# The head's modulation in columns: weights stationary, one column of c moving

## The chip, the cores and the metric

The kernel runs on one core of one Trainium2 chip. The metric is the device time of one execution in microseconds (us). A core has five engines that run their own queues in order and wait for each other by semaphores: PE (TensorE, the matrix engine; PEld is its loading of weights), DVE (VectorE), ACT (ScalarE), POOL (GpSimd) and SP (SyncE, which here issues nearly all DMA transfers).

## The reference

Two transformer blocks follow each other on 256 tokens of 1024 columns, all in f32. The part that the change touches is the start of the first block: a modulation vector computed from `c`, and the first gated feed-forward layer.

```python
c_act = jax.nn.silu(c)                                                       # (1, 1024)
mod = (einsum('bd,dn->bn', c_act, w_ada[l]) + b_ada[l]).reshape(b, 3, 3, 1024)
h = rms_norm(x, norm_w[l, 0]) * (1 + mod[:, 0, 1]) + mod[:, 0, 0]            # modulate
x = x + 0.5 * mod[:, 0, 2] * swiglu(h, ffn_w13[l, 0], ffn_w2[l, 0])
# swiglu: g, u = split(h @ w13); (silu(g) * u) @ w2, with 2816 columns of g and of u
```

A mixer with attention and convolution, a second feed-forward layer and the second block follow; `p_2` is an input of the second block, which the kernel transposes early.

## The kernel before

Everything is kept transposed: columns of the model on the 128 partitions, the 256 tokens along the free axis. A product of two f32 matrices is made of three fast products (`mm3`, lines 154 to 156): both operands are split into a rounded part `hi` (ACT, a cast) and the rest `lo` (DVE, a subtraction), by `hilo` (L178, L179) or `split` (L143, L144). In the tables below `gu` is the bank in which g and u of the first feed-forward layer are summed, `acc` that of its second product.

**The head.** `x` comes in, is transposed raw (`xt_ps<-ident,x_nat`) and, once its row norm is known, normed (`xn`). The modulation vector has 9216 columns, of which the first layer needs shift (0 to 1023) and scale (1024 to 2047) at once. They are computed in four blocks of 512 columns: `ada_start(0)` and `ada_start(8)` are shift and scale of the model's first 512 columns, `ada_start(4)` and `ada_start(12)` of the last 512 (the number is the column in units of 128). I call them blocks 0, 8, 4 and 12. Of a block, the 1024 rows of `w_ada` lie as 128 partitions x 8 terms, two tiles `ada` of four terms (1 MB each). Before, terms 0, 1, 4 and 5 are multiplied by their value of c and added up by DVE (`ada_acc`, L216 and L218); terms 2, 3, 6 and 7 go to PE with c as the stationary operand, broadcast over 128 columns, and 512 columns of weights moving (L221); one more product with a matrix of ones adds `ada_acc` over the partitions (L223). The result stands 128 times in a bank `ada_ps`; DVE picks its diagonal, 128 columns at a time, by a multiplication with the identity and a sum (L226, four times), and adds the bias (L228), into columns of `modT`. `ada_scale` (L199) turns the scale into `aT`.

**The first strip.** The first layer goes over 11 strips of 256 columns of g and u. The first strip's weights come in two halves of four terms (`strips_half`), and `h_half(i)` makes four terms of the modulated input h: nu (L592, ACT: `xn` times `aT` plus `modT`), hh and hl (its two parts), and the casts of the half strip between. `gemm_half(i)` multiplies: per term 2 output groups x 2 (g, u) x 3 products. So the strip is 8 terms x 12 = 96 products of 256 columns, and then the second strip's 96 follow (`i = 1` in `swiglu`), then the first down strip.

**What sets the order.** The code is written in the order below; a scheduler in the framework then orders each engine's instructions by its own estimate of when their inputs are there, unless `issue_after` ties one behind another. On the chip each engine goes through its queue strictly in that order. SP's queue issues the transfers in order too; seven tiles `ada` can be held, so the eighth waits for the first. `then` is a list of small jobs, one behind each strip: `vector_columns` loads nine small vectors (`rowB`) and transposes them, `transpose_p` transposes `p_2`.

```python
    ada_start(0, (0, 1, 4, 5))
    ada_start(8, (0, 1, 4, 5))
    strips_half(0)
    h_half(0)
    ada_start(4, (0, 1, 4, 5))
    ada_start(12, (0, 1, 4, 5))
    gemm_half(0)
    strips_half(4)
    h_half(4)
    gemm_half(4)
```

Of the kernel before, what the change touches and what calls it, by code (L numbers as in the profile page):

```python
# [8 lines left out]
F32 = mybir.dt.float32  # L9
# [4 lines left out]
ALU = mybir.AluOpType  # L14
# [4 lines left out]
P = 128  # L19
T = 256  # L20
D = 1024
KD = D // P
# [39 lines left out]
def tile_two_blocks(ctx: ExitStack, tc: tile.TileContext, t: dict, out: bass.AP):  # L62
    nc = tc.nc
    vec, act, pe, sync, pool = nc.vector, nc.scalar, nc.tensor, nc.sync, nc.gpsimd
# [12 lines left out]
    def bankB(name):  # L77
        return psB.tile([P, 512], F32, tag="ps", name=name)
# [21 lines left out]
    start = tc.tile_pool(name="start", bufs=1)  # L100
    start_ctx, start = start, start.__enter__()
# [7 lines left out]
    ident = const.tile([P, P], F32, name="ident")  # L109
# [5 lines left out]
    ones = {}  # L115
# [49 lines left out]
    def gemm_many(jobs, x, kc, ks=None):  # L165

        for k in ks or range(kc):
            for i, (ps, w, c0) in enumerate(jobs):
                mm3(ps, w[0][:, k, c0:c0 + P], w[1][:, k, c0:c0 + P], x[0][:, k, :], x[1][:, k, :],
                    k == 0 and i % 2 == 0, k == kc - 1)  # L170
# [6 lines left out]
    def hilo(src, hi, lo):  # L177
        act.copy(hi, src)  # L178
        vec.tensor_tensor(out=lo, in0=src, in1=hi.bitcast(F32), op=ALU.subtract)  # L179

    def tr(dst, src, n=P):
        pe.transpose(out=dst, in_=src, identity=ident[:n, :n])
# [5 lines left out]
    c_act = const.tile([P, 8], F32, name="c_act")  # L188
    tab(c_act, c_raw, AF.Silu)
    modT = const.tile([P, 72], F32, name="modT")  # L190
    aT = const.tile([P, 24], F32, name="aT")
    gT = const.tile([P, 24], F32, name="gT")
    colA = const.tile([P, 96], F32, name="colA")
    xT = res.tile([P, KD, T], F32, name="xT")
    w_ada = t["w_ada"][0].rearrange("(p k) n -> p k n", k=8)
# [3 lines left out]
        vec.scalar_tensor_tensor(out=aT[:, s * 8 + ci:s * 8 + ci + n], in0=modT[:, s * 24 + 8 + ci:s * 24 + 8 + ci + n],  # L199
                                 scalar=1.0, in1=colA[:, 72 + s * 8 + ci:72 + s * 8 + ci + n], op0=ALU.add, op1=ALU.mult)  # L200

    def ada_start(ci, mine):

        parts = []
        for k0 in (0, 4):
            w = start.tile([P, 2048], F32, tag="ada", name="ada", bufs=7)
            wv = w.rearrange("p (k n) -> p k n", k=4)
            sync.dma_start(out=wv, in_=w_ada[:, k0:k0 + 4, ci * P:ci * P + 512])
            parts += [wv[:, k, :] for k in range(4)]
        acc = start.tile([P, 512], F32, tag="ada_acc", name="ada_acc", bufs=2)  # L210
        b = bankB("ada_ps")
        begun = False
        for k in range(8):
            if k in mine:
                if k == mine[0]:
                    vec.tensor_scalar_mul(acc, parts[k], c_act[:, k:k + 1])  # L216
                else:
                    vec.scalar_tensor_tensor(out=acc, in0=parts[k], scalar=c_act[:, k:k + 1], in1=acc,  # L218
                                             op0=ALU.mult, op1=ALU.add)
            else:  # L220
                pe.matmul(b, lhsT=c_act[:, k:k + 1].to_broadcast([P, P]), rhs=parts[k], start=not begun, stop=False)  # L221
                begun = True
        pe.matmul(b, lhsT=ones[1], rhs=acc, start=False, stop=True)  # L223
        for i in range(4):
            junk = start.tile([P, P], F32, tag="junk", name="junk", bufs=2)
            vec.tensor_tensor_reduce(out=junk, in0=b[:, i * P:(i + 1) * P], in1=ident, scale=1.0, scalar=0.0,  # L226
                                     op0=ALU.mult, op1=ALU.add, accum_out=modT[:, ci + i:ci + i + 1])
        vec.tensor_tensor(out=modT[:, ci:ci + 4], in0=modT[:, ci:ci + 4], in1=colA[:, ci:ci + 4], op=ALU.add)  # L228


    colB = const.tile([P, 64], F32, name="colB")
# [2 lines left out]
    def vector_columns():  # L234
        rowB = tmp.tile([P, P], F32, tag="nu", name="rowB")
        vec.memset(rowB[32:64, :], 1.0)
        at = 0
        for name, v in (("mix", t["norm_mix_g_2"][0]), ("mlp", t["norm_mlp_g_2"][0]), ("ple", t["norm_ple_g_2"][0]),
                        ("bg", t["b_gate_2"][0]), ("qa", t["q_a_norm"][0]), ("kva", t["kv_a_norm"][0]),
                        ("cw", t["conv_w"][0].rearrange("j c -> (j c)"))):  # L240
            n = v.shape[0] // P
            sync.dma_start(out=rowB[at:at + n], in_=v.rearrange("(r c) -> r c", c=P))
            col_at[name] = at
            at += n
        for name, a in (("mq", t["q_norm_nope"]), ("mk", t["k_norm_nope"])):
            sync.dma_start(out=rowB[at:at + 1, 0:64], in_=a)
            col_at[name] = at
            at += 1
        b = bankB("col_ps2")
        tr(b[:, 0:at], rowB[0:at, :], at)  # L250
        vec.tensor_copy(colB[:, 0:at], b[:, 0:at])
# [74 lines left out]
    def drain(g):  # L326
        for _ in g:
            pass
# [43 lines left out]
    def h_tiles():  # L372
        return (res.tile([P, KD, T], F32R, tag="hh", name="hh"), res.tile([P, KD, T], F32R, tag="hl", name="hl"))
# [150 lines left out]
    def transpose_p():  # L524
        pnat = tmp.tile([P, 2, 256], F32, tag="pnat", name="pnat", bufs=1)
        sync.dma_start(out=pnat, in_=t["p_2"][0][0].rearrange("(k p) n -> p k n", p=P))
        b = bankB("pT")
        for c in range(2):
            for tk in range(2):
                tr(b[:, c * T + tk * P:c * T + (tk + 1) * P], pnat[:, tk, c * P:(c + 1) * P])  # L530
        hilo(b, flat(pH), flat(pL))
# [16 lines left out]
    for tk in range(2):  # L548
        junk = start.tile([P, D], F32, tag="xn", name="junk", bufs=2)
# [18 lines left out]
    b = bankB("col_ps")  # L568
# [4 lines left out]
    h = h_tiles()  # L573

    h = h_tiles()
    rope_steps = rope_table()
# [5 lines left out]
    first = [bankB("gu") for _ in range(2)]  # L582
# [12 lines left out]
                for z in range(2):  # L595
                    hilo(part(raw[z], k, 2), part(hi[z], k, 2), part(lo[z], k, 2))

    def gemm_half(i):
        gemm_many([(b[:, z * T:(z + 1) * T], (whole(hi[z]), whole(lo[z])), j * P) for j, b in enumerate(first)
                   for z in range(2)], h, KD, range(i, i + 4))  # L600

    ada_start(0, (0, 1, 4, 5))
    ada_start(8, (0, 1, 4, 5))
    strips_half(0)
    h_half(0)
    ada_start(4, (0, 1, 4, 5))
    ada_start(12, (0, 1, 4, 5))
    gemm_half(0)
    strips_half(4)
    h_half(4)  # L610
    gemm_half(4)
    start_ctx.__exit__(None, None, None)
    swiglu(h, t["ffn_w13"][0][0], t["ffn_w2"][0][0], gt(0), ada_rest(ada_plan[:8], (0, 0, 1, 1, 1, 1, 1, 1, 1, 1)),
           then=(lambda: None, vector_columns, transpose_p, lambda: next(rope_steps), lambda: None,
                 lambda: drain(rope_steps)), first=first, at=(16, 16))
    mid = ada_rest(ada_plan[8:12], (1,), halves=False)


# [331 lines left out]
    h = modulated(nw(2), sh(2))  # L950
# [310 lines left out]
    h, make_rb = gained("mlp")  # L1261
# [20 lines left out]
    with tc.tile_pool(name="px3", bufs=1) as px:  # L1282
# [5 lines left out]
        h, _ = gained("ple", sums=False)  # L1288
        w = t["w_ple_gate_2"][0]
# [17 lines left out]
        for c in range(2):  # L1307
            for tk in range(2):
                junk = px.tile([P, 512], F32, tag="junk", name="junk", bufs=2)
# [49 lines left out]
        for s in range(2):  # L1359
            b = bankB("pg")  # L1360
# [9 lines left out]
        for part, (c0, n) in enumerate(((0, 512), (512, T), (768, T))):  # L1370
            b = bankB("pg")
# [83 lines left out]
```

## Time and profile before

| | |
|---|---|
| median of 3 runs | 1011.21 us |
| lowest, highest | 1010.92, 3466.13 us |
| the profiled execution's time | 1011.66 us |
| its span, first to last instruction | 1009.9 us |
| PE busy | 983.6 us, 97% of the span |
| weight loads busy | 948.8 us, 94% |
| DVE busy | 745.8 us, 74% |
| ACT busy | 557.9 us, 55% |
| mean granted clock of PE | 0.994 of full |

The profile comes from one execution. Times of instructions are counted from the start of its span; what the device time has beyond the span, 1.76 us, lies around it. A timeline row has the start in us, the duration (of the whole group, where several instructions are merged), the engine, the line, the operation with output and inputs, how many, and in brackets how long the engine had been idle before and what ended that. A duration of PE runs from a product's start to its modelled end, so products overlap, and the distance between starts tells what one costs in a stream.

### The profile page before, as it was taken

How to read it: one execution, taken by the hardware profiler on the slowest of the kernel's cores; microseconds unless marked ns; L12 is line 12 of the kernel's file. 1: busy time of each engine (PE TensorE's matmuls, PEld its weight loads, DVE VectorE, ACT ScalarE, POOL GpSimd, SP SyncE). 2: the span in 40 equal slices, each digit the busy share in tenths (PEclk: the TensorE clock that was granted, in tenths of full speed). 3: DMA queues.
4: the chain of work that ended last, by engine and by line, in shares of the span. 5: the costliest groups of instructions: out<-in, count | busy, mean ns of one | idle time of the engine just before them, and what ended most of it. 6: DMA issues, size and time to landing. Idle time of an engine off the chain costs nothing.

```text
span 1009.9 us, 20118 instructions
## 1 busy us (share of the span) xinstructions
PE 983.6 (97%) x8244; PEld 948.8 (94%) x8244; DVE 745.8 (74%) x1430; ACT 557.9 (55%) x1032; POOL 30.2 (3%) x42
## 2 busy tenths in 40 slices
PE   6999999999999998999999999999999999999996
PEld 3799999999988997999999999999999999999996
DVE  4889999847976999796454679986577885655664
ACT  5654545547765655645444555554566774554555
POOL 0000000010000001000000010001000100000000
PEclk9999999999999998999999999999999999999999
DMA  9899999726574888996563454535545896565411
GB/s 343 283 373 355 332 313 316 267 88 188 169 229 127 258 306 266 321 345 201 177 206 128 126 161 129 173 126 159 161 124 170 264 309 194 192 190 195 160 63 42
DMA packets 159330, 215.28 MB, mean 213 GB/s; under 512 B 6350, under 2 KB 125925, under 8 KB 159110
## 3 DMA queue, kind: packets, MB, share of 16 engines
q1 hardware_dynamic: 157442, 212.58, 63.8%
q10 hardware_dynamic: 1796, 1.42, 0.4%
q8 instruction: 64, 1.05, 0.4%
q14 instruction: 28, 0.23, 0.1%
HBM read 210.51 MB, written 3.47 MB: 212 GB/s over the span
## 4 chain that ended last, share of the span: by engine, by line
PE 79%; DVE 12%; ACT 4%; DMA 3%; issue 2%; SPq 0%; DVEq 0%; ACTq 0%
PE gu L154 8%; PE gu L156 8%; PE gu L155 8%; PE acc L154 7%; PE acc L155 7%; PE acc L156 6%; DVE lo L144 4%; PE u L154 3%; PE u L155 3%; PE u L156 3%; ACT hi L143 2%; DMA ada<-in_w_ada_dram 1%; PE gab L156 1%; DVE ada_acc L274 1%; PE gab L154 1%
## 5 line engine op out<-in xcount | busy, mean ns | idle before, releaser
L144 DVE TENSOR_TENSOR lo<-raw,hi 128x512 fp32r<-128x512 f32 (+2 forms) x454 | 395.2, 900 | 84.1 <-ACT hi L143 83.1
L143 ACT CAST hi<-raw 128x512 fp32r<-128x512 f32 (+2 forms) x454 | 337.0, 786 | 173.4 <-PE acc L155 51.3
L154 PE MATMUL gu<-hh,hi 128*128 128x256 f32 x704 | 198.1, 282 | 3.0 <-ACT hh L385 3.0
L156 PE MATMUL gu<-hh,lo 128*128 128x256 f32 x704 | 195.8, 279 | 0.2 <-DVE lo L144 0.2
L155 PE MATMUL gu<-hl,hi 128*128 128x256 f32 x704 | 195.4, 278 | 0.0
L155 PE MATMUL acc<-ml,hi 128*128 128x256 f32 x608 | 168.0, 277 | 0.4 <-DVE ml L179 0.4
L154 PE MATMUL acc<-mh,hi 128*128 128x256 f32 x608 | 167.9, 278 | 0.3 <-ACT mh L178 0.3
L156 PE MATMUL acc<-mh,lo 128*128 128x256 f32 x608 | 167.8, 277 | 0.0
L154 PEld LDWEIGHTS gu<-hh,hi 128*128 128x128 f32 x704 | 133.5, 190 | 3.6 <-ACT hh L385 3.1
L156 PEld LDWEIGHTS gu<-hh,lo 128*128 128x128 f32 x704 | 133.3, 190 | 0.5 <-DVE lo L144 0.4
L155 PEld LDWEIGHTS gu<-hl,hi 128*128 128x128 f32 x704 | 133.3, 190 | 0.5 <-issue 0.5
L154 PEld LDWEIGHTS acc<-mh,hi 128*128 128x128 f32 x608 | 113.9, 188 | 0.9 <-ACT mh L178 0.7
L155 PEld LDWEIGHTS acc<-ml,hi 128*128 128x128 f32 x608 | 114.0, 188 | 0.8 <-DVE ml L179 0.8
L156 PEld LDWEIGHTS acc<-mh,lo 128*128 128x128 f32 x608 | 114.1, 188 | 0.0
L274 DVE SCALAR_TENSOR_TENSOR ada_acc<-ada,c_act,ada_acc 128x512 f32<-128x512 f32 x98 | 73.4, 749 | 2.1 <-DMA ada<-in_w_ada_dram 0.3
L154 PE MATMUL u<-hh,hi 128*128 128x256 f32 x256 | 71.0, 277 | 0.0
L155 PE MATMUL u<-hl,hi 128*128 128x256 f32 x256 | 70.8, 277 | 0.0
L156 PE MATMUL u<-hh,lo 128*128 128x256 f32 x256 | 70.8, 276 | 0.0
L88 ACT ACTIVATE s<-gu 128x256 f32<-128x256 f32 x44 | 16.6, 379 | 68.3 <-PE gu L156 68.1
L154 PEld LDWEIGHTS u<-hh,hi 128*128 128x128 f32 x256 | 48.1, 188 | 0.0
L155 PEld LDWEIGHTS u<-hl,hi 128*128 128x128 f32 x256 | 48.0, 188 | 0.0
L156 PEld LDWEIGHTS u<-hh,lo 128*128 128x128 f32 x256 | 48.1, 188 | 0.0
(404 smaller groups left out, 2154.0 us busy)
## 6 DMA issues: line engine op xcount, KB each, us to landing
raw<-in_ffn_w_dram SPq DMA_DIRECT2D x64, 1024.0 KB
raw<-in_w_in_dram SPq DMA_DIRECT2D x37, 1024.0 KB
raw<-in_w_ff_dram SPq DMA_DIRECT2D x32, 1024.0 KB
ada<-in_w_ada_dram SPq DMA_DIRECT2D x28, 1024.0 KB
raw<-in_w_out_dram SPq DMA_DIRECT2D x8, 1024.0 KB
ada<-in_w_ada_dram SPq DMA_DIRECT2D x8, 768.0 KB
raw<-in_w_branch_dram SPq DMA_DIRECT2D x8, 512.0 KB
raw<-in_w_out_a_dram SPq DMA_DIRECT2D x4, 1024.0 KB
```

The source lines that it names most:

```text
L88: last_table[0] = act.activation(*args, **kw).ins
L143: act.copy(hi[:, sl], raw[:, sl])
L144: vec.tensor_tensor(out=lo[:, sl], in0=raw[:, sl], in1=hi[:, sl].bitcast(F32), op=ALU.subtract)
L154: pe.matmul(ps, lhsT=wh, rhs=xh, start=start, stop=False, skip_group_check=True)
L155: pe.matmul(ps, lhsT=wh, rhs=xl, start=False, stop=False, skip_group_check=True)
L156: pe.matmul(ps, lhsT=wl, rhs=xh, start=False, stop=stop, skip_group_check=True)
L274: vec.scalar_tensor_tensor(out=acc, in0=wv[:, k, :], scalar=c_act[:, k0 + k:k0 + k + 1], in1=acc, op0=ALU.mult, op1=ALU.add)
```

## The change

`ada_start` now gives the first four terms of a block to DVE and the last four to PE. On PE the weights are the stationary operand, 128 columns at a time, and one column moves: c's value of that term (or a column of ones for `ada_acc`). The result comes as one column per group of 128, four columns of the bank, so the diagonal is no longer read; DVE adds the bias right from the bank. The second tile of block 12 comes in two transfers. The first strip's products are cut 3 + 1 + 4 terms in place of 4 + 4: three terms ahead of blocks 4 and 12, the fourth tied behind block 12's last product. `transpose_p` moves from behind the third strip to behind the second, beside `vector_columns`.

```diff
-    def ada_start(ci, mine):
-
-        parts = []
+    def ada_start(ci, rows=4):
+
+
+        wv = []
         for k0 in (0, 4):
...
+            n = rows if k0 else 4
+            for k in range(0, 4, n):
+                sync.dma_start(out=w[:, k:k + n, :], in_=w_ada[:, k0 + k:k0 + k + n, ci * P:ci * P + 512])
+            wv += [w[:, k, :] for k in range(4)]
         acc = start.tile([P, 512], F32, tag="ada_acc", name="ada_acc", bufs=2)
+        for k in range(4):
+            if k == 0:
+                vec.tensor_scalar_mul(acc, wv[0], c_act[:, 0:1])
+            else:
+                vec.scalar_tensor_tensor(out=acc, in0=wv[k], scalar=c_act[:, k:k + 1], in1=acc, op0=ALU.mult, op1=ALU.add)
         b = bankB("ada_ps")
...
-                pe.matmul(b, lhsT=c_act[:, k:k + 1].to_broadcast([P, P]), rhs=parts[k], start=not begun, stop=False)
-                begun = True
-        pe.matmul(b, lhsT=ones[1], rhs=acc, start=False, stop=True)
-        for i in range(4):
-            junk = start.tile([P, P], F32, tag="junk", name="junk", bufs=2)
-            vec.tensor_tensor_reduce(out=junk, in0=b[:, i * P:(i + 1) * P], in1=ident, scale=1.0, scalar=0.0,
-                                     op0=ALU.mult, op1=ALU.add, accum_out=modT[:, ci + i:ci + i + 1])
-        vec.tensor_tensor(out=modT[:, ci:ci + 4], in0=modT[:, ci:ci + 4], in1=colA[:, ci:ci + 4], op=ALU.add)
+        terms = [(acc, ones[1][:, 0:1])] + [(wv[k], c_act[:, k:k + 1]) for k in range(4, 8)]
+        for n, (w, v) in enumerate(terms):
+            for j in range(4):
+                last = pe.matmul(b[:, j:j + 1], lhsT=w[:, j * P:(j + 1) * P], rhs=v, start=n == j == 0, stop=n == 4,
+                                 skip_group_check=True)
+        vec.tensor_tensor(out=modT[:, ci:ci + 4], in0=b[:, 0:4], in1=colA[:, ci:ci + 4], op=ALU.add)
+        return last.ins
...
-    def gemm_half(i):
+    def gemm_part(i, n):
...
-                   for z in range(2)], h, KD, range(i, i + 4))
-
-    ada_start(0, (0, 1, 4, 5))
-    ada_start(8, (0, 1, 4, 5))
+                   for z in range(2)], h, KD, range(i, i + n))
+
+    ada_start(0)
+    ada_start(8)
     strips_half(0)
     h_half(0)
-    ada_start(4, (0, 1, 4, 5))
-    ada_start(12, (0, 1, 4, 5))
-    gemm_half(0)
+    gemm_part(0, 3)
+    ada_start(4)
+    with tc.issue_after(ada_start(12, rows=2)):
+        gemm_part(3, 1)
     strips_half(4)
     h_half(4)
-    gemm_half(4)
+    gemm_part(4, 4)
...
-           then=(lambda: None, vector_columns, transpose_p, lambda: next(rope_steps), lambda: None,
-                 lambda: drain(rope_steps)), first=first, at=(16, 16))
+           then=(lambda: None, lambda: (vector_columns(), transpose_p()), lambda: None, lambda: next(rope_steps),
+                 lambda: None, lambda: drain(rope_steps)), first=first, at=(16, 16))
```

What the scheduler makes of it on DVE, between the norm of x and the first parts of h, before (block 0's reading of the diagonal, `ISA junk,modT`, and block 8's products; `waits PE_49` is a wait for PE):

```order
L216 TENSOR_SCALAR ada_acc<-ada,c_act 128x512 [waits DMAHW1_49]
L218 SCALAR_TENSOR_TENSOR ada_acc<-ada,c_act,ada_acc 128x512 [waits DVE_49]
L226 ISA junk,modT<-ada_ps,ident 128x128 [waits PE_49]
L226 ISA modT 128x1
...
L228 TENSOR_TENSOR modT<-modT,colA 128x4 [waits DVE_49]
L218 SCALAR_TENSOR_TENSOR ada_acc<-ada,c_act,ada_acc 128x512 [waits DMAHW2_49]
```

and after, from the end of block 0's products to the end of block 12 (L224 is the addition of the bias, L215 and L217 are the products):

```order
L224 TENSOR_TENSOR modT_100<-ada_ps_196,colA_103 128x4 [waits PE_49]
L215 TENSOR_SCALAR ada_acc_222<-ada_218,c_act_98 128x512 [waits DMAHW1_49]
L217 SCALAR_TENSOR_TENSOR ada_acc_222<-ada_218,c_act_98,ada_acc_222 128x512 [waits DVE_49] x3
L224 TENSOR_TENSOR modT_100<-ada_ps_227,colA_103 128x4 [waits PE_49]
L199 SCALAR_TENSOR_TENSOR aT_101<-modT_100,colA_103 128x4 [waits DVE_49]
...
L179 TENSOR_TENSOR hl_178<-nu_272,hh_177 128x256 [waits Activation_49]
L215 TENSOR_SCALAR ada_acc_316<-ada_312,c_act_98 128x512 [waits DMAHW5_49]
L217 SCALAR_TENSOR_TENSOR ada_acc_316<-ada_312,c_act_98,ada_acc_316 128x512 [waits DVE_49] x3
L224 TENSOR_TENSOR modT_100<-ada_ps_321,colA_103 128x4 [waits PE_49]
L215 TENSOR_SCALAR ada_acc_348<-ada_343,c_act_98 128x512 [waits DMAHW7_49]
```

All four products of a block now stand behind the wait for the block before it (two of them did before), and blocks 4 and 12 stand behind the last hl of the first half of h, where before block 4's first product stood among the parts of the strip.

On ACT, behind the two normings of x, before (the casts of the half strip, then nu):

```order
L178 CAST hi<-raw 128x512 [waits DMAHW3_49]
L178 CAST hi<-raw 128x512
L178 CAST hi<-raw 128x512 [waits DMAHW4_49]
L178 CAST hi<-raw 128x512
L592 ACTIVATE nu<-xt_ps,modT,aT 128x256 [waits DVE_49,PE_49]
```

and after (nu is L589 there):

```order
L589 ACTIVATE nu<-xt_ps,modT,aT 128x256 [waits DVE_49,PE_49]
L589 ACTIVATE nu<-xt_ps,modT,aT 128x256
L178 CAST hh<-nu 128x256 [waits Activation_49]
L178 CAST hi<-raw 128x512 [waits DMAHW3_49]
L178 CAST hh<-nu 128x256 [waits Activation_49]
```

The casts have moved from ahead of nu to behind it, and so behind its wait for DVE.

On PE the products of blocks 4 and 12 stood ahead of the first gu products and among them; after, 36 gu products come first, then the two blocks, the second behind the first:

```order
L156 MATMUL gu<-hh,lo 128x256
L222 MATMUL ada_ps<-ones_92,ada_acc 128x1 [waits DVE_49,PE_49]
L222 MATMUL ada_ps<-ones_92,ada_acc 128x1 x3
L222 MATMUL ada_ps<-c_act,ada 128x1 [waits DMAHW6_49]
L222 MATMUL ada_ps<-c_act,ada 128x1 x15
L222 MATMUL ada_ps<-ones_92,ada_acc 128x1 [waits DVE_49,PE_49]
```

A block is 20 products in the program, 4 of `ada_acc` and 16 of the tile.

## Rows read from the trace of the kernel before

**Rows 1.** Windows: busy us by engine, clock, DMA share, GB/s.

```profile
20.00:24.00 4.00, 1.54 (x5) 0.50 (x4) 3.22 (x14) 2.01 (x5) 0.00 (x0) 1.00 1.05 387
...
36.00:40.00 4.00, 4.00 (x38) 4.00 (x37) 3.14 (x15) 1.78 (x6) 0.00 (x0) 1.00 0.60 159
```

**Rows 2.** Timeline of PE: start, us, what; head of the program.

```profile
23.89 1.95 PE L221 MATMUL ada_ps<-ada,c_act 128*128 128x512 f32 x4 [2.46 <-DMA ada<-in_w_ada_dram]
...
31.60 0.68 PE L154 MATMUL gu<-hh,hi 128*128 128x256 f32 x1
...
35.23 0.69 PE L154 MATMUL gu<-hh,hi 128*128 128x256 f32 x1
...
45.40 0.28 PE L156 MATMUL gu<-hh,lo 128*128 128x256 f32 x1
```

**Rows 3.** Timeline of weight loads, same columns.

```profile
11.79 0.19 PEld L221 LDWEIGHTS ada_ps<-ada,c_act 128*128 128x128 f32 x1 [0.43 <-issue]
...
13.54 0.14 PEld L182 LDWEIGHTS xt_ps<-ident,xn 128*128 128x128 f32 x1 [0.26 <-ACT xn L557]
```

**Rows 4.** Source L221: min/median/max ns of one.

```profile
L221 PEld LDWEIGHTS ada_ps<-ada,c_act x32: 185/190/338, 10.0 to 33.9; 128*128 128x128 f32 x32
L221 PE MATMUL ada_ps<-ada,c_act x32: 590/592/1193, 10.0 to 34.3; 128*128 128x512 f32 x32
```

**Rows 5.** Timeline of weight loads, 393 to 396 us.

```profile
394.73 0.52 PEld L909 LDWEIGHTS bias_ps<-hot,wide_tabs 33*128 33x128 f32 x4 [0.33 <-DVE lo L144]
```

**Rows 6.** Source L285: loads of bf16 weights, one column moving.

```profile
L285 PEld LDWEIGHTS <-ada_b x168: 95/96/100, 96.9 to 496.0; 128*128 128x128 bf16 x168
L285 PE MATMUL ada_ps<-one,ada_b x168: 163/163/178, 96.9 to 496.0; 128*128 128x1 bf16 x168
```

**Rows 7.** Timeline of PE, 98 us.

```profile
98.46 0.40 PE L285 MATMUL ada_ps<-one,ada_b 128*128 128x1 bf16 x10
```

**Rows 8.** Source L1187: loads of 64 columns.

```profile
L1187 PEld LDWEIGHTS bob<-pT,vB x64: 132/137/137, 703.2 to 730.9; 128*64 128x64 f32 x64
```

**Rows 9.** Timeline of PE, at 6 us.

```profile
6.01 3.62 PE L182 MATMUL xt_ps<-ident,x_nat 128*128 128x128 f32 x16
```

**Rows 10.** Timeline of PE, from 398 us.

```profile
398.33 1.23 PE L154 MATMUL gu<-hh,hi 128*128 128x256 f32 x4 [2.98 <-ACT hh L385]
...
399.79 0.41 PE L154 MATMUL gu<-hh,hi 128*128 128x256 f32 x1
400.00 0.41 PE L155 MATMUL gu<-hl,hi 128*128 128x256 f32 x1
```

**Rows 11.** Windows around a fall of the clock (columns as in rows 1).

```profile
397.00:398.00 1.00, 0.00 (x0) 0.00 (x0) 0.96 (x3) 0.23 (x1) 0.00 (x0) 0.70 1.11 332
...
404.00:405.00 1.00, 1.00 (x10) 1.00 (x9) 1.00 (x2) 0.21 (x1) 0.00 (x0) 0.88 0.38 82
```

**Rows 12.** Timeline of DVE, head of the program.

```profile
15.35 0.49 DVE L216 TENSOR_SCALAR ada_acc<-ada,c_act 128x512 f32<-128x512 f32 x1 [1.09 <-DMA ada<-in_w_ada_dram]
...
17.18 0.29 DVE L226 CUSTOM_DVE_ANT_0 junk<-ada_ps,ident 128x128 f32<-128x128 f32 x1 [0.56 <-PE ada_ps L223]
...
18.15 0.16 DVE L228 TENSOR_TENSOR modT<-modT,colA 128x4 f32<-128x4 f32 x1
...
27.74 1.53 DVE L218 SCALAR_TENSOR_TENSOR ada_acc<-ada,c_act,ada_acc 128x512 f32<-128x512 f32 x2
29.21 0.49 DVE L216 TENSOR_SCALAR ada_acc<-ada,c_act 128x512 f32<-128x512 f32 x1
29.74 0.75 DVE L218 SCALAR_TENSOR_TENSOR ada_acc<-ada,c_act,ada_acc 128x512 f32<-128x512 f32 x1
```

**Rows 13.** Timeline of ACT, head of the program.

```profile
19.58 1.14 ACT L178 CAST hi<-raw 128x512 fp32r<-128x512 f32 x2 [6.09 <-DMA raw<-in_ffn_w_dram]
...
23.85 1.02 ACT L592 ACTIVATE nu<-xt_ps,modT,aT 128x256 f32<-128x256 f32 x2 [1.63 <-DVE aT L199]
...
25.72 1.02 ACT L592 ACTIVATE nu<-xt_ps,modT,aT 128x256 f32<-128x256 f32 x2 [0.25 <-DVE hl L179]
```

More of the change, by code (lines that the diff above doesn't have):

```diff
@@ L200, in ada_scale @@
                                  scalar=1.0, in1=colA[:, 72 + s * 8 + ci:72 + s * 8 + ci + n], op0=ALU.add, op1=ALU.mult)
-    def ada_start(ci, mine):
-        parts = []
+    def ada_start(ci, rows=4):
+        wv = []
         for k0 in (0, 4):
[L206 to L209, printed above, removed]
-        acc = start.tile([P, 512], F32, tag="ada_acc", name="ada_acc", bufs=2)
-        b = bankB("ada_ps")
[L212 to L220, printed above, removed]
-                pe.matmul(b, lhsT=c_act[:, k:k + 1].to_broadcast([P, P]), rhs=parts[k], start=not begun, stop=False)
-                begun = True
-        pe.matmul(b, lhsT=ones[1], rhs=acc, start=False, stop=True)
-        for i in range(4):
-            junk = start.tile([P, P], F32, tag="junk", name="junk", bufs=2)
-            vec.tensor_tensor_reduce(out=junk, in0=b[:, i * P:(i + 1) * P], in1=ident, scale=1.0, scalar=0.0,
-                                     op0=ALU.mult, op1=ALU.add, accum_out=modT[:, ci + i:ci + i + 1])
-        vec.tensor_tensor(out=modT[:, ci:ci + 4], in0=modT[:, ci:ci + 4], in1=colA[:, ci:ci + 4], op=ALU.add)
@@ new lines, in ada_start @@
+            w = start.tile([P, 2048], F32, tag="ada", name="ada", bufs=7).rearrange("p (k n) -> p k n", k=4)
+            n = rows if k0 else 4
+            for k in range(0, 4, n):
+                sync.dma_start(out=w[:, k:k + n, :], in_=w_ada[:, k0 + k:k0 + k + n, ci * P:ci * P + 512])
+            wv += [w[:, k, :] for k in range(4)]
+        acc = start.tile([P, 512], F32, tag="ada_acc", name="ada_acc", bufs=2)
+        for k in range(4):
[3 more added lines that the diff above has]
+                vec.scalar_tensor_tensor(out=acc, in0=wv[k], scalar=c_act[:, k:k + 1], in1=acc, op0=ALU.mult, op1=ALU.add)
```

## The prediction

> **What bounds the kernel now.** I read the windows first. From 36 us on PE is busy without a gap, and the whole program keeps it busy [rows 1]; only the head has holes, such as the 1.54 us of work in 20 to 24 us. So a change in the head is worth what it moves the point from which PE runs on. The timeline of PE shows that point: the first gu product starts at 31.60, the stream that no longer stops at 35.23, and the last product of the first strip starts at 45.40 [rows 2], so the first strip ends at 45.5. What lies behind is the same work before and after. I therefore follow one thing: when does the first strip end?
>
> In the head DMA runs at a share of 1.05 in 20 to 24 us [rows 1], and the third ada block's first half is there at 23.89 [rows 2]. The old code is fitted to these landings: PE multiplies tiles as they land, and DVE its share beside it.
>
> **What a block costs PE.** Before, a block is four products of 512 columns and one with ones. The 16 products of L221 in the program are 32 weight loads and 32 matmuls in the trace [rows 4]: two passes for each f32 product. A pass of 512 columns adds about 0.43 us at full clock: 592 ns from start to end, less the 163 ns that a product with one column takes [rows 4, 6]. Ten passes make 4.3 us for a block.
>
> After, a block is 5 terms x 4 column groups = 20 products, by the same splitting 40 passes, each a load of 128x128 f32 and one moving column. The column costs next to nothing, so the load is the price. The trace of before has no f32 load with one column behind it. The nearest row is four f32 loads with 128 and 32 columns behind them: 0.52 us for four [rows 5], of which the last takes some 0.19 (a load of L221 is 190 ns [rows 4]), so (0.52 - 0.19)/3 = 0.11 us from load to load. The lower bound are bf16 loads with one column: ten in 0.40, of which the last takes 0.163, so 0.026 us each [rows 6, 7]. I take 0.11: the f32 load is longer than the bf16 one by 190 - 96 = 94 ns, and one of 64 f32 columns takes 137 [rows 8], so 64 columns more cost 53 ns, 128 some 106. A block is then 40 x 0.111 = 4.4 us, no less than before.
>
> The Trainium skill, page "TensorE: Matmul & The Clock Gate", section "Back-to-back issue gap", lists about 25 ns as the floor from product to product for 1 to 64 columns; by that a block would be 1.0 us and the time that of the second rival below, about 1009. Rows 5 and 8 speak against it, rows 7 for it. The Trainium skill, page "FP8 and Floating Point Precision", section "TensorE Precision Notes", has four passes for true FP32; if each loaded weights, a block would be 8.9 us and the time about 1040. The trace shows two loads for a product [rows 4].
>
> **The clock.** The head starts at half clock: 16 transposes of 128 columns take 3.62 us from 6.01 [rows 9], (3.62 - 0.42)/15 = 0.213 each, and gu products at half clock also stand 0.21 apart [rows 10]. Before, the wide L221 products follow at 10.0 [rows 4], and by 11.79 a load takes 0.19 us in place of the longest's 0.338 [rows 3, 4]: full clock, some 1.8 us after they began. The change takes just these away: PE has nothing until xn. Later in the trace PE idled for 2.98 us, the clock fell to half at about 397.4, and it came back only at about 404.2, 5.9 us after products of 256 columns had begun at 398.33 [rows 10, 11]. No row shows whether loads with one column behind them keep or raise the clock. From both sides: a pass costs 0.111 or 0.214. I take half clock for a stretch that holds nothing but narrow passes, since the array then streams almost no columns; what that is worth the other way is a rival.
>
> **The chain after.** The order of DVE matters more than the price. After, DVE waits for PE's block 0 (the addition into modT) ahead of block 8's products, and again for block 4 ahead of block 12's, where before it had half of them done. DVE's four products take 27.74 to 29.21 for two, 0.53 and 0.75 for the others, in all 2.75 us [rows 12]. Queued behind the first wait is all of h_half(0), and PE waits for that. ACT too has the casts of the strip now behind nu, so that they no longer fill the time before aT: in before two casts ran from 19.58, and nu waited until 23.85 [rows 13]. h_half(0) costs four nu and four hh, 1.62 us for two of each without the 0.25 us wait (23.85 to 25.72 [rows 13]), and four casts at about 0.55: with the wait 5.5 us, and 0.3 for the last hl, 5.8 in all.
>
> At half clock, in us: the transposes of xn can go on from 13.54 [rows 3], 12 x 0.214, to 16.1. Block 0: 8.6, to 24.7. modT, then DVE's products for block 8 (landed since 15.35 [rows 12]): 0.2 + 2.75, to 27.6. Block 8: 8.6, to 36.2. modT and aT: 0.4, to 36.6. h_half(0): to 42.4; PE runs gemm_part(0, 3) in it, from about 38.5 to 44.5, and I let the clock rise some 4 us after they begin, between the 1.8 and the 5.9 above. DVE's products for block 4: 2.75, to 45.1. Block 4: mostly at full clock, falling at its end, 4.8, to 49.9. modT and block 12's products: 3.0, to 52.9. Block 12, after 2.9 us of idle and narrow passes before: 8.6, to 61.5. gemm_part(3, 1), 12 products at 0.214: 64.1. h_half(4) from 61.9 to 67.7, and 48 products beside it, at half clock to 66.3, 4.8 us after the wide products began again, and then 0.1135 apart: the strip ends at **70.6**. That is 25.1 us after 45.5.
>
> With full clock all the way the same chain is 14.8 (xn), 19.3, 22.2, 26.7, 27.1 (aT), 32.9 (h_half), 35.6, 40.1, 43.1, 47.6, and 53.7 for h_half(4); the strip ends at 56.1, 10.6 us late.
>
> **The other edits.** DVE loses 16 readings of the diagonal: a block's reading went from 17.18 to 18.31 [rows 12], 1.13 us, and is 0.16 now. I have counted it: modT is 0.2 in the chain. Two transfers for the last tile in place of one let half of its products begin earlier; the tile has long landed by 52.9, so it is worth nothing here, and one more issue on SP costs nothing while SP is ahead. p's transposes move by one strip: four on PE as before, one hi and one lo of 128x512 on ACT and DVE; they lie beside the second strip's stream and cost nothing, or with that cover gone about 1.2 us. The transfer of the first down strip no longer waits for the diagonal's reading but now stands behind the nine small rows and p, and rowB waits on DVE until the end of h_half(4); the strip is needed after some 11 us of the next products, so nothing waits. Up to 1 us may come back, since the next strip's casts are done before the first ends.
>
> **The rivals.** *Narrow passes raise and hold the clock.* Loads follow each other without a gap, which speaks for it; transposes at 6 us ran 3.6 us without raising it [rows 9], which speaks against. The chain then ends between 56.1, full all along, and 60.3, with half clock through xn's transposes (1.3 us) and for 27 of the 80 passes of blocks 0 and 8, before the clock first rises and after the idle between them (27 x 0.103 = 2.8): 10.6 to 14.8 us late, 1022 to 1026. *The load hides* (not slower): f32 loads with one column follow at the pace of the bf16 ones, 0.026. A block is 1.1 us, the chain ends at 42.7 at full clock, 2.8 early, or 1 to 2 late with the wide products at half clock: 1009 to 1013. It decides at 0.044 us for a pass, where 160 passes x (0.044 - 0.026) eat the 2.8. Rows 5 and 8 speak against. *The change does not do what it says*: a one-column product is split in more passes than two. Double loads make 17.8 us more at full clock, about 1040; rows 4 speak against.
>
> **How the numbers follow.** The profiled execution took 1011.66, 0.45 over the median 1011.21 of the runs; the third run, 3466.13, is not a time of this work. 1011.66 + 25.1 = 1036.8, less the 0.45: 1036. Chances: half clock 0.50 (1031 to 1042 with 5 us either way for where the clock turns), clock held 0.33, the load hides 0.14, more passes 0.03. The range 1013 to 1042 leaves out most of the third case and the edge of the first, under 2 in 10. Two per cent, what a measurement of this kernel can tell from no change, is 20.2 us: slower by more holds nine tenths of the first case and the last, 0.47; faster by more has no case, 0.01; within, 0.52.
>
> **What would show it.** Right: loads of ada over 0.2 us apart and a granted clock of 0.5 in blocks 0, 8 and 12; ada_acc of block 8 starting only after block 0's last product; the first gu after 35 us, the last of the first strip near 70. Wrong: loads 0.03 apart; a granted clock of 1.0 through all four blocks; or DVE's products for blocks 8 and 12 running ahead of modT, against the order. Behind the first strip I expect equal times; a difference there of more than 3 us would be one that I did not see.

## The result and the profile after

The changed kernel takes 1036.1 us (median of 4 runs, 1033.97 to 1038.04), the kernel before beside it 1011.2 (median of three, 1010.92 to 1014.96, with a fourth run of 3466.13 left out as before). The ratio is 1.0242 with a 95% interval of 1.0222 to 1.0262: slower, and by just over two per cent. The profiled execution took 1035.83 us with a span of 1034.0, and its mean granted clock is 0.975 where before it was 0.994.

The timeline of PE, changed kernel, head of the program (L222 are the products of `ada_start`; x8 are the passes of `ada_acc`, x32 those of the tile):

```profile
13.14 2.82 PE L182 MATMUL xt_ps<-ident,xn 128*128 128x128 f32 x12 [0.38 <-ACT xn L554]
15.75 1.31 PE L222 MATMUL ada_ps<-ones,ada_acc 128*128 128x1 f32 x8
16.92 4.25 PE L222 MATMUL ada_ps<-c_act,ada 128*128 128x1 f32 x32
24.27 1.84 PE L222 MATMUL ada_ps<-ones,ada_acc 128*128 128x1 f32 x8 [3.10 <-DVE ada_acc L217]
25.97 6.96 PE L222 MATMUL ada_ps<-c_act,ada 128*128 128x1 f32 x32
...
35.32 0.58 PE L154 MATMUL gu<-hh,hi 128*128 128x256 f32 x1 [2.38 <-ACT hi L178]
...
42.16 1.02 PE L222 MATMUL ada_ps<-ones,ada_acc 128*128 128x1 f32 x8
43.04 3.71 PE L222 MATMUL ada_ps<-c_act,ada 128*128 128x1 f32 x32
49.85 1.84 PE L222 MATMUL ada_ps<-ones,ada_acc 128*128 128x1 f32 x8 [3.10 <-DVE ada_acc L217]
51.55 6.96 PE L222 MATMUL ada_ps<-c_act,ada 128*128 128x1 f32 x32
...
68.20 0.28 PE L156 MATMUL gu<-hh,lo 128*128 128x256 f32 x1
```

Four blocks can be read off, one behind the other, in order 0, 8, 4, 12. The same 32 passes take 3.71 us in block 4, 4.25 in block 0 and 6.96 in blocks 8 and 12: (3.71 - 0.25)/31 = 0.112 us a pass in the one, (6.96 - 0.35)/31 = 0.213 in the others (0.25 and 0.35 are what one pass lasts, below). Ahead of blocks 8 and 12 PE idles 3.10 us for DVE. The first strip's last product starts at 68.20, before at 45.40 [rows 2]: 22.8 us late.

The source view of L222, changed kernel (min/median/max ns of one):

```profile
L222 PEld LDWEIGHTS ada_ps<-c_act,ada x128: 192/333/333, 16.9 to 58.1; 128*128 128x128 f32 x128
L222 PE MATMUL ada_ps<-c_act,ada x128: 250/352/352, 16.9 to 58.2; 128*128 128x1 f32 x128
L222 PEld LDWEIGHTS ada_ps<-ones,ada_acc x32: 186/333/338, 15.5 to 51.3; 128*128 128x128 f32 x32
...
who waited for it (us, times):
  DVE modT L224: 31.3, 4
```

160 loads for 80 products: two a product, as the wide form had [rows 4]. A load lasts 0.19 us at full clock, as in [rows 4], and 0.333 at half. DVE waits 31.3 us at the four additions into modT.

Windows of the changed kernel (columns as in [rows 1]; the third last is the granted clock):

```profile
16.00:17.00 1.00, 1.00 (x8) 1.00 (x8) 0.00 (x0) 0.00 (x0) 0.00 (x0) 0.75 1.07 370
...
19.00:20.00 1.00, 1.00 (x11) 1.00 (x10) 0.00 (x0) 0.00 (x0) 0.00 (x0) 0.95 1.09 370
20.00:21.00 1.00, 1.00 (x6) 1.00 (x6) 0.00 (x0) 0.00 (x0) 0.00 (x0) 0.50 1.07 391
20.00:24.00 4.00, 1.17 (x6) 1.08 (x6) 2.69 (x5) 0.00 (x0) 0.00 (x0) 0.50 1.05 386
36.00:40.00 4.00, 4.00 (x21) 4.00 (x21) 3.70 (x8) 2.76 (x7) 0.00 (x0) 0.50 0.10 33
40.00:41.00 1.00, 1.00 (x9) 1.00 (x9) 0.96 (x2) 0.00 (x0) 0.00 (x0) 0.81 0.00 0
47.00:48.00 1.00, 0.00 (x0) 0.00 (x0) 0.96 (x2) 0.00 (x0) 0.00 (x0) 0.61 0.00 0
64.00:65.00 1.00, 1.00 (x9) 1.00 (x9) 0.89 (x3) 1.00 (x2) 0.00 (x0) 0.86 0.84 202
```

The clock comes up to its upper level (2.4 GHz) about 16.5, in block 0, behind the dense transposes of xn. It falls back to half (1.2 GHz) about 19.9, while PE is busy all the time with one-column passes, and comes back about 40.4, 5 us into the gu products; it falls again about 47.2, after block 4, and comes back about 64.3. Where 36 to 40 us before was a stretch of 38 products without a gap [rows 1], it is one of 21 now: PE is "busy" at half clock. DMA has nothing left to bring there (0.10 against 0.60): the weights have long landed, and what holds the head back is PE and the order of its neighbours.

The order, in the timeline of DVE and then of ACT, changed kernel:

```profile
21.21 0.16 DVE L224 TENSOR_TENSOR modT<-ada_ps,colA 128x4 f32<-128x4 f32 x1 [8.84 <-PE ada_ps L222]
21.29 0.48 DVE L215 TENSOR_SCALAR ada_acc<-ada,c_act 128x512 f32<-128x512 f32 x1
...
39.16 0.48 DVE L215 TENSOR_SCALAR ada_acc<-ada,c_act 128x512 f32<-128x512 f32 x1
```

```profile
33.43 1.02 ACT L589 ACTIVATE nu<-xt_ps,modT,aT 128x256 f32<-128x256 f32 x2 [20.35 <-DVE aT L199]
```

Block 8's products start on DVE at 21.29, right behind the addition that waited 8.84 us for PE; their tile was there by 15.35 before [rows 12]. nu starts at 33.43, where it was 23.85 [rows 13], and ACT had idled 20.35 us ahead of it with the casts queued behind.

### The profile page after: what moved, and what is told of

It reads as the page before. It is cut to its first block, busy times and chain, and to the rows that moved or that the text cites. A ratio compares the mean times of both kernels' runs of the same rounds, so it can differ in the third digit from the quotient of the medians.

```text
span 1034.0 us, 20324 instructions
## 1 busy us (share of the span) xinstructions
PE 999.8 (97%) x8364; PEld 975.6 (94%) x8364; DVE 743.3 (72%) x1398; ACT 558.1 (54%) x1032; POOL 30.2 (3%) x42
## 4 chain that ended last, share of the span: by engine, by line
PE 78%; DVE 13%; ACT 4%; DMA 3%; issue 2%; SPq 0%; DVEq 0%; ACTq 0%
PE gu L154 8%; PE gu L155 8%; PE gu L156 8%; PE acc L154 6%; PE acc L155 6%; PE acc L156 6%; DVE lo L144 4%; PE ada_ps L222 3%; PE u L154 2%; PE u L155 2%; PE u L156 2%; DMA ada<-in_w_ada_dram 2%; PE gab L156 1%; PE gab L154 1%; PE gab L155 1%
## 5 line engine op out<-in xcount | busy, mean ns | idle before, releaser
L154 PE MATMUL gu<-hh,hi 128*128 128x256 f32 x704 | 200.2, 285 | 5.5 <-ACT hh L382 3.0
L155 PE MATMUL gu<-hl,hi 128*128 128x256 f32 x704 | 197.8, 282 | 0.0
L155 PEld LDWEIGHTS gu<-hl,hi 128*128 128x128 f32 x704 | 135.9, 193 | 0.0
```

The source lines that it names most:

```text
L154: pe.matmul(ps, lhsT=wh, rhs=xh, start=start, stop=False, skip_group_check=True)
L155: pe.matmul(ps, lhsT=wh, rhs=xl, start=False, stop=False, skip_group_check=True)
```

## The experiments

No kernel here leaves out a part of the computation. "Last product" is the start of the 96th gu product in the timeline: 45.40 before, 68.20 after.

**The change in two parts.** First the columns alone, in the old program:

```diff
-    ada_start(0, (0, 1, 4, 5))
-    ada_start(8, (0, 1, 4, 5))
+    ada_start(0)
+    ada_start(8)
...
-    ada_start(4, (0, 1, 4, 5))
-    ada_start(12, (0, 1, 4, 5))
+    ada_start(4)
+    ada_start(12)
     gemm_half(0)
```

> The columns alone: the new ada_start in the old program, with the strip's products 4 + 4 and p's transposes where they were. The theory of the prediction (a pass costs a load, 0.111 us at full clock and 0.213 at half, and the additions into modT hold the next block's products on DVE): the loss is all in ada_start, so the first strip ends 20 to 24 us after 45.5 and the time is 1032 to 1037. Rival A (the cut 3 + 1 + 4 makes the loss, since it puts two blocks between PE and the fourth term): the strip ends under 55, time 1012 to 1021. Rival B (moving p's transposes costs): under 2 us less than the changed kernel, which only the two us behind the first strip could hold.

Measured: 1044.7 us, ratio 1.0311 (1.0284 to 1.0338); last product at 78.94, 33.5 us late. The columns hold the whole loss, and more: without the rest of the change it is larger, by 8.6 us by the times and by 7 by the ratios, which neither the theory nor a rival had. (The runs stand beside different runs of the kernel before, whose medians lie between 1010.8 and 1012.9 us, so a ratio is the safer measure of a difference.) PE of this kernel:

```profile
17.96 6.96 PE L222 MATMUL ada_ps<-c_act,ada 128*128 128x1 f32 x32
...
45.90 1.84 PE L222 MATMUL ada_ps<-ones,ada_acc 128*128 128x1 f32 x8 [9.21 <-DVE ada_acc L217]
47.60 6.96 PE L222 MATMUL ada_ps<-c_act,ada 128*128 128x1 f32 x32
...
59.37 0.56 PE L154 MATMUL gu<-hh,hi 128*128 128x256 f32 x1
```

All four blocks run at 0.213 us a pass, and the first gu product comes within block 12. In the changed kernel the 36 products of `gemm_part(0, 3)` stand ahead of block 4, fill PE's wait for DVE and bring the clock back: block 4 took 4.6 us there (42.16 to 46.75) and takes 8.7 here (45.90 to 54.56). So the cut 3 + 1 + 4 is a gain beside one-column blocks. The windows of this run are a warning:

```profile
48.00:52.00 4.00, 4.00 (x20) 4.00 (x20) 0.00 (x0) 0.00 (x0) 0.00 (x0) 1.00 0.00 0
```

20 passes in 4 us are half clock, yet the column says 1.00, and the mean clock of the run is 0.997, higher than before's, in the slowest kernel of all. The clock had not once changed up to 70 us, and ahead of the first change in the record the column seems to have nothing to go by: in two later runs too it reads 1.00 over whole blocks at 0.213 us a pass. The distance between products is the safer clock.

Then all but the columns: the changed kernel with before's `ada_start` (512 columns moving, diagonal read). Against its expectation one edit is missing: `rows` is taken here but not used, so the second tile of block 12 comes in one transfer as before.

```diff
-    def ada_start(ci, rows=4):
+    def ada_start(ci, mine=(0, 1, 4, 5), rows=4):
...
-        terms = [(acc, ones[1][:, 0:1])] + [(wv[k], c_act[:, k:k + 1]) for k in range(4, 8)]
+                pe.matmul(b, lhsT=c_act[:, k:k + 1].to_broadcast([P, P]), rhs=parts[k], start=not begun, stop=False)
+        last = pe.matmul(b, lhsT=ones[1], rhs=acc, start=False, stop=True)
```

> Everything of the change but the columns: 512 columns of weights moving and the diagonal read as before, with the cut 3 + 1 + 4, the second tile of block 12 in two transfers, and p's transposes moved. The theory of the prediction: these edits cost nothing by themselves; the first strip ends between 45 and 49, time 1011 to 1017. Rival A (the cut makes the loss): the strip ends near 60 or later, time over 1025. Rival B (moving p costs): strip end as before, but some 2 us more behind it.

Measured: 1013.7 us, ratio 1.0006 (0.9987 to 1.0025). Last product at 48.09, 2.7 us late, most of which comes back behind the strip. Cut and p cost nothing that the interval shows; rivals A and B fall. The two transfers were not tried by themselves.

**Clock and order.** 128 columns of c in place of one take the half clock away if narrow passes are its cause, without changing the loads:

```diff
-        terms = [(acc, ones[1][:, 0:1])] + [(wv[k], c_act[:, k:k + 1]) for k in range(4, 8)]
+        terms = [(acc, ones[1])] + [(wv[k], c_act[:, k:k + 1].to_broadcast([P, P])) for k in range(4, 8)]
...
-                last = pe.matmul(b[:, j:j + 1], lhsT=w[:, j * P:(j + 1) * P], rhs=v, start=n == j == 0, stop=n == 4,
+                last = pe.matmul(b[:, j * P:(j + 1) * P], lhsT=w[:, j * P:(j + 1) * P], rhs=v, start=n == j == 0, stop=n == 4,
```

> The changed kernel with c's value broadcast to 128 moving columns in place of one: the same weight loads, the same number of passes, output groups of 128 columns of which the addition reads the first. The scheduler's order changes with it: DVE has block 8's products ahead of the first addition into modT, and the casts of the strip come ahead of nu. So both suspects, the clock and the order, are taken away together. The theory of the prediction (a pass costs the load, 0.11 at full clock, and one column more or 128 more does not matter to it; at half clock it is 0.21, because narrow passes don't hold the clock): 128 columns hold the clock, blocks take 4.5 us each, the strip ends at 46 to 50, time 1012 to 1017. Rival C (the stationary weights are the loss, whatever the clock and the order): the strip ends over 60, time over 1027. Rival D (128 columns run at half clock as well, and only the order helps): strip end 55 to 60, time 1021 to 1026.

Measured: 1014.4 us, ratio 1.0018 (1.0001 to 1.0036), last product at 49.85. 128 times as many columns move, and nearly 22 us are back; rivals C and D fall. But the scheduler's order changed as well. So the order alone, with one column: on DVE each block's products are tied ahead of the addition into modT of the block before it, and on ACT the casts come ahead of nu.

```diff
+            with tc.issue_after(after) if after and k == 0 else nullcontext():
...
+    p0 = ada_products(0)
+    p8 = ada_products(8)
+    ada_columns(0, p0, after=p8[2])
     strips_half(0)
+    casts(0)
+    p4 = ada_products(4)
+    ada_columns(8, p8, after=p4[2])
     h_half(0)
     gemm_part(0, 3)
...
+    p12 = ada_products(12, rows=2)
+    ada_columns(4, p4, after=p12[2])
...
```

> One column moving as in the changed kernel, but the order written out by hand: DVE has block 8's products ahead of the first addition into modT, block 4's ahead of the second and block 12's ahead of the third, and the casts of the half strip come ahead of nu on ACT. The theory of the prediction (clock and order each make a part): the blocks of one column still run at half clock, some 8.6 us each where the one before fed no wide product, and only the waits go, 3 us at block 8, 2.5 at h_half(0), 3 at block 4 and 12: the first strip ends at 56 to 60, time 1022 to 1027. Rival E (the order alone makes the loss): the strip ends at 46 to 50, time 1012 to 1017. Rival F (the clock alone makes the loss): the strip ends at 65 to 68 as in the changed kernel, time 1032 to 1037.

Measured: 1026.2 us, ratio 1.0122 (1.0096 to 1.0149), last product at 59.65. Neither the order alone (rival E) nor the clock alone (rival F). The two cells that complete the square keep 128 columns (the edit above, with `terms` as there) under either order, held by hand. The early order has the lines just shown; the late one has:

```diff
+    p0 = ada_products(0)
+    a0 = ada_columns(0, p0)[1]
+    p8 = ada_products(8, after=a0)
+    ada_columns(8, p8)
     strips_half(0)
     h_half(0)
     gemm_part(0, 3)
+    p4 = ada_products(4, after=last_lo[0])
+    a4 = ada_columns(4, p4)[1]
+    p12 = ada_products(12, rows=2, after=a4)
...
```

> 128 columns of c moving and the early order written out by hand (the products of the next block ahead of each addition into modT, the casts ahead of nu). A candidate for a version that beats both: DVE no longer reads the diagonal. By the theory the blocks' price on PE is that of before (40 loads, 4.4 us, against 4.3), so little is to be gained: the first strip's last product between 45 and 49.9, time 1011 to 1014. If the freed DVE time were worth something, it would be under 1009.

> 128 columns of c moving, but with the order of the changed kernel held by hand: block 8's products on DVE behind the first addition into modT, the casts behind nu, block 4's products behind the last hl of the first half of h, block 12's behind the addition for block 4 (some other DVE work comes ahead of the last addition, which the changed kernel had behind it). This is the fourth cell beside the changed kernel (one column, late order), the one with one column and the early order (1026.2) and the one with 128 columns and the early order (1014.4). If clock and order each cost their part and add up, the order costs here what it costs at one column, 1036.1 - 1026.2 = 9.9 us on 1014.4: time 1022 to 1026, the first strip's last product near 58 to 60, and the granted clock full in the blocks. Rival G (the order costs only because the blocks are long at half clock): under 1018. Rival H (the order is the loss, and 128 columns helped only by way of it): over 1032.

Measured, with the ratio and its interval:

| | early order | late order |
|---|---|---|
| one column | 1026.2 us, 1.0122 (1.0096 to 1.0149) | the change, 1036.1, 1.0242 (1.0222 to 1.0262) |
| 128 columns | 1015.1 us, 1.0031 (1.0018 to 1.0044) | 1028.5, 1.0166 (1.0148 to 1.0183) |

The two kernels with the early order have the same instructions in the same order on PE, DVE and ACT until block 4; only the moving columns differ (behind that the scheduler put some casts of later strips elsewhere). Timeline of PE and windows, first with one column, then with 128:

```profile
13.91 2.82 PE L184 MATMUL xt_ps<-ident,xn 128*128 128x128 f32 x12 [0.38 <-ACT xn L563]
...
23.53 6.96 PE L230 MATMUL ada_ps<-c_act,ada 128*128 128x1 f32 x32
...
39.77 3.71 PE L230 MATMUL ada_ps<-c_act,ada 128*128 128x1 f32 x32
...
19.00:20.00 1.00, 1.00 (x11) 1.00 (x11) 0.00 (x0) 0.47 (x1) 0.00 (x0) 1.00 1.10 373
20.00:21.00 1.00, 1.00 (x9) 1.00 (x8) 0.00 (x0) 0.66 (x2) 0.00 (x0) 0.69 1.05 382
21.00:22.00 1.00, 1.00 (x6) 1.00 (x7) 0.00 (x1) 0.97 (x2) 0.00 (x0) 0.50 1.05 387
```

```profile
21.64 3.74 PE L230 MATMUL ada_ps<-c_act,ada 128*128 128x128 f32 x32
...
20.00:21.00 1.00, 1.00 (x12) 1.00 (x11) 0.05 (x1) 0.65 (x3) 0.00 (x0) 1.00 1.05 387
21.00:22.00 1.00, 1.00 (x12) 1.00 (x11) 1.00 (x3) 0.54 (x2) 0.00 (x0) 1.00 1.05 387
```

In the first PE has no gap from 13.91 until block 8 ends at 30.49, loads follow loads, and still the clock falls about 20.4. With 128 columns it stays up. Block 8's tile takes 6.96 us in the one (at 23.53) and 3.74 in the other (at 21.64). Where one column ran at full clock, in block 4 (at 39.77), the tile took 3.71: a pass of 128 columns is hardly dearer than one of a single column. This is the cleanest test of the clock's cause. At the early order it is worth 1026.2 - 1015.1 = 11.1 us by the times, and 9 to 10 by the ratios (1.0122 here, 1.0133 in the second run below, against 1.0031).

The lower right cell came out 2.5 us above its bound, with the last product at 64.54 in place of 58 to 60:

```profile
24.35 2.04 PE L230 MATMUL ada_ps<-ones,ada_acc 128*128 128x128 f32 x8 [3.10 <-DVE ada_acc L220]
26.18 5.82 PE L230 MATMUL ada_ps<-c_act,ada 128*128 128x128 f32 x32
...
51.04 2.05 PE L230 MATMUL ada_ps<-ones,ada_acc 128*128 128x128 f32 x8 [5.12 <-DVE pos_f L506]
52.88 4.48 PE L230 MATMUL ada_ps<-c_act,ada 128*128 128x128 f32 x32
```

I had expected full clock in all blocks. But the waits of the late order let it fall, and blocks 8 and 12 begin at half. Within them it comes back (the tile takes 5.82 and 4.48, not 6.96), which it did in no one-column block behind such a wait. And 2 us of the 5.12 are other DVE work ahead of block 12's last products. So clock and order are not cleanly two separate causes: a wait costs its own time and then the clock. In time they nearly add up all the same: by the ratios the late order costs 14 us with 128 columns, 2 of them that other work, and 11 to 12 with one. Rivals G and H fall, the time lies between them.

The cell with 128 columns and the early order is no win over before (1.0031, a little over what was expected): its last product is at 49.07, 3.7 us late, and no gain shows from the DVE time that the diagonal no longer takes. The last cut is 128 columns in the old program, the edit of `terms` upon the columns alone:

> The columns alone in the old program (the strip cut 4 + 4, p's transposes where they were), with 128 columns of c moving. With one column this was 1044.7, 8.6 us over the changed kernel: there the first gu products came only behind block 12, at 59.4, and every block ran at half clock. If the clock was the reason, 128 columns bring all of it back: time 1011 to 1016, the first strip's last product at 45 to 49. If the cut 3 + 1 + 4 is needed whatever the clock, the time is 1019 to 1024.

Measured: 1018.0 us, ratio 1.0054 (1.0038 to 1.0070), last product at 50.83: 1044.7 - 1018.0 = 26.7 us are back. Not by the clock alone: as with the first run of 128 columns, the scheduler's order changed too. Block 8's products now run on DVE from 15.01, ahead of the first addition into modT (with one column from 25.04, behind it), and the casts run ahead of nu, so this run does not tell the two apart. The time lies between the two bounds: PE waits 4.20 us for block 4's products and enters them at half clock (the first eight passes take 1.84 us, block 12's 1.05):

```profile
29.40 1.84 PE L222 MATMUL ada_ps<-ones,ada_acc 128*128 128x128 f32 x8 [4.20 <-DVE ada_acc L217]
```

**Work added to hold the clock.** In the kernel with one column and the early order, blocks 8 and 12 get ten useless products of 128 columns each, 20 in all:

```diff
+                if ci > 7 and j % 2:
+                    pe.matmul(b[:, P:2 * P], lhsT=ident, rhs=ident, start=False, stop=n == 4, skip_group_check=True)
```

> The kernel with one column moving and the early order (1026.2), with useless work added on PE in the blocks that ran at half clock: in blocks 8 and 12, behind every second product, one more f32 product of 128 columns, the identity with itself, into columns of the bank that nobody reads; 20 products, 40 passes of 0.11 us at full clock. Nothing is taken away, so the one-column passes, the loads and the order stay as they are. If the one column is what lets the clock fall, PE is given columns to stream and holds full clock: block 8 takes 4.4 + 2.2 = 6.6 us in place of 8.6, block 12 6.6 in place of 7.7, and the gu products behind both run at full clock from their start, some 3 us and 1.7 us: time 1017 to 1021. If the loss is the price of the passes whatever the clock, the added passes cost their 4.4 us or more on the path: time over 1029.

> The kernel with one column and the early order once more, to stand beside the one with the added products on the same chip: 1024 to 1028.

Measured: 1034.6 us, ratio 1.0241 (1.0211 to 1.0272), beside 1024.8, ratio 1.0133 (1.0106 to 1.0160), for the same without. My expectation failed. The filled kernel, timeline of PE in blocks 0 and 8, then a window in block 12:

```profile
17.19 6.97 PE L230 MATMUL ada_ps<-c_act,ada 128*128 128x1 f32 x32
...
28.00 0.85 PE L230 MATMUL ada_ps<-c_act,ada 128*128 128x1 f32 x4
28.71 0.78 PE L233 MATMUL ada_ps<-ident 128*128 128x128 f32 x2
29.28 0.85 PE L230 MATMUL ada_ps<-c_act,ada 128*128 128x1 f32 x4
```

```profile
52.00:56.00 4.00, 4.00 (x21) 4.00 (x21) 0.00 (x0) 0.00 (x0) 0.00 (x0) 0.50 0.98 318
```

Six passes, four of one column and two of 128, take 1.28 us, 0.213 each. But PE entered both blocks at half clock: block 0 had run at it throughout (6.97 us at 17.19), and the clock fell about 48.7, at the end of block 4's one-column passes, just ahead of block 12. So the passes in between did not bring the clock back; whether they would have held it, this run does not show. The time lies in the range that I had given to the other reading (over 1029), but its reason is not shown either: 40 passes at 0.213 us make 8.5 of the 9.8 us between the two kernels, and they cost that much because the clock was at half. That speaks neither for nor against the square above.

## Why the prediction came out

The time, 1036, and the direction were right. The range, 1013 to 1042, had room for the second case too (the clock held, 1022 to 1026), so the steps tell more than the total. Forecast and measured (us):

| step | forecast | measured |
|---|---|---|
| xn's transposes end | 16.1 | 16.0 |
| block 0 ends | 24.7 | 21.2 |
| block 8 begins, ends | 27.6, 36.2 | 24.3, 32.9 |
| last hl of `h_half(0)` | 42.4 | 39.2 |
| block 4 begins, ends | 45.1, 49.9 | 42.2, 46.8 |
| block 12 begins, ends | 52.9, 61.5 | 49.9, 58.5 |
| the strip ends, late against before | 25.1 | 22.8 |

**The price of a pass** held: 0.111 said, 0.112 measured, and 0.213 at half. With one column moving the load paces it, as the same price with 128 columns shows. 512 columns add 0.43 us to a pass [rows 4], so 128 add some 0.107 (an estimate): there columns and load cost about the same, and more columns would set the price. The Trainium skill, page "TensorE: Matmul & The Clock Gate", section "Back-to-back issue gap", has about 25 ns as the floor there. The bf16 passes with one column come to it (0.026, [rows 7]); with an f32 load for each pass no run came near it, so the rival that hung on it (the load hides) is out by a factor of four.

**Half clock in narrow stretches** held for blocks 8 and 12, and the square shows it as a cause of the loss. The rival in which the narrow passes hold the clock falls with the fall about 20.4 in mid-stream. The Trainium skill, same page, section "Part 1: The HAM clock gate", puts the lower level down to idleness; the run shows the fall with PE and its loads busy for 1.00 of every window, and the measurement decides.

**The order** held: it is worth 10 us with one column by the times (1036.1 to 1026.2), 11 to 12 by the ratios, and 13 to 14 with 128, 2 of those other work.

**The term that was mis-sized is block 0:** 8.6 said, 5.4 measured (15.75 to 21.17), since the clock rose behind xn's transposes and served 3.4 us of it. I had seen only transposes that did not raise it [rows 9]. This is not fixed: in the run of the columns alone and in the second run with one column and the early order block 0 took its 8.5 us. The latter's PE:

```profile
15.54 1.71 PE L230 MATMUL ada_ps<-ones,ada_acc 128*128 128x1 f32 x8
17.11 6.96 PE L230 MATMUL ada_ps<-c_act,ada 128*128 128x1 f32 x32
```

In the first run of that same kernel the tile's passes took 4.41. So 3 us of this head depend on the execution, about as much as the runs of the changed kernel spread (4.1 us; that the clock makes that spread is not shown, since only one of them left a trace). Smaller, and the other way: the clock came back 5.9 us after the wide products behind block 12 began (58.38 to 64.3), where I had 4.8, which is worth some 0.5 us (an estimate, half of the difference). Two slips of the working changed little: four nu and hh with four casts make 5.44 us without the 0.25 us wait, so `h_half(0)` is 6.0 and not 5.8; and 2.8 us under 1011.2 is 1008, not 1009.

**Behind the strip** I had said equal times, with up to 1 us back. The span is 24.1 us longer, 1.3 more than the strip's 22.8, so a strip 2.3 us better than forecast and a loss behind it that I had not forecast partly cancel: that the total met 1036 so closely is luck. 1.3 us do come back by the mixer (its first `lat` product starts at 249.9, before at 228.4: 21.5 late). Then PE idles 0.91 us ahead of 390.79 for a cast of ACT, 0.24 before, and about 1.3 us more come between 420 and 465, with no further idle. The windows there and, for comparison, later, changed kernel:

```profile
440.00:460.00 20.00, 20.00 (x172) 20.00 (x172) 19.11 (x25) 10.44 (x16) 0.00 (x0) 1.00 1.03 353
...
540.00:560.00 20.00, 20.00 (x179) 20.00 (x178) 9.45 (x12) 8.90 (x13) 0.00 (x0) 1.00 0.62 208
```

172 products of 256 columns in place of 179 in 20 us, 4% fewer, at a granted clock of 1.00. Before had 179 in the same part of the program (420 to 460). What makes such a stretch is open.

## What to carry to other kernels

Turning a product round, so that the weights stand and a vector moves, saves columns but not loads: with f32 weights a pass cost 0.11 us, as its load did, whether 1 or 128 columns moved, so count loads before columns. Dense passes of one column lost PE its full clock here in mid-stream (about 19.9 in the changed kernel, 20.4 with the early order), and what was wide behind blocks 8 and 12 started at half clock; block 4, entered at full clock, ended before the fall in the changed kernel. Broadcasting the vector to 128 columns cost next to nothing and kept the clock where PE did not wait; 512 columns added 0.43 us to a pass [rows 4]. A diff that removes work from an engine can still lengthen its waits: read the new queue order of every engine that waits for the edited step, and put what needs nothing ahead of what waits.

## What I had not expected

- The granted clock fell about 20.4 us in the kernel with one column and the early order although PE had had no gap since 13.91; in the trace of before the fall that I had read came behind idle time (2.98 us in [rows 10]).
- 128-column passes among twice as many one-column passes left PE at the half clock that it came with, 0.213 us a pass, through the 13 us of block 8 in the filled kernel (24.02 to 37.17).
- The kernel with the worst clock shows the best mean (0.997): ahead of the first recorded change the column reads 1.00, whatever the products' distance says.
- Stretches of some 40 us in which products stand 4% further apart at a granted clock of 1.00: 172 against 179 in 20 us.
